# Hi/lo activation halves side by side in one 512-column product, low parts two ticks later, and w_up's row scale on VectorE

## Chip, cores and metric

The kernel runs on one core of a Trainium2 chip. The metric is the device time of one execution in microseconds; the median of three runs is given.

## The reference

One decoder block on 256 tokens of width 1024: a pooling mixer beside causal attention in 8 heads of 64, then cross attention with 4 heads of 256 on 256 memory tokens, then a feed-forward part of width 2816 with a causal convolution of three taps. All in float32.

```python
h = rms_norm(x, norm_mix_g); proj = h @ w_in                  # 1024 x 2048: pool part, q, k, v
x = x + concat([pool(u), attention(q, k, v)]) @ w_out
h = rms_norm(x, norm_xattn_g); m = rms_norm(mem, norm_mem_g)
q = rms_norm(h @ w_xq); k, v = split(m @ w_xkv); k = rms_norm(k)
x = x + softmax(q k^T / 16) v @ w_xo
h = rms_norm(x, norm_ffn_g)
up = conv3_causal(h @ w_up) + conv_b                          # 1024 x 5632
gate, val = split(up)
x = x + (silu(gate) * val) @ w_down                           # 2816 x 1024
```

## The kernel before, in words

Every large product keeps float32 accuracy with two-part operands: a value is a high part (rounded to the TensorE form fp32r) plus a low part (the rest), and a product is high x high + high x low + low x high. `split_h` (L186, ScalarE cast, L194) and `split_l` (L196, VectorE difference, L205) make both parts of a weight unit of 128x1024; `need(u)` (L207) calls them for units ahead of the one in use, by `look[0]` units. `LOOKS` sets that number for each stage, and `HOLD` sets it to 0 for the last tiles of a residual stage (3 tiles in the first, 1 in the second), so that the splits kept back come out in one go at the next stage's first `need`. Raw weights come by DMA in chunks of two units through three buffers.

There are two kinds of stages. In the first kind (`a_chunk`, L359: w_in and w_xkv) the activations are the stationary operand and 512 columns of weights stream. In the second kind, with transposed output (`b_tile`, L701: w_out, w_xq, w_xo, w_up, w_down), a 128x128 block of weights is stationary, the 256 tokens stream, and the output has its features on the partitions. There a block is three products of 256 columns by `three` (L263 to L267). One tile of 128 output features is 8 blocks (22 in w_down), accumulated in one PSUM bank or half of one. w_up runs 22 pairs of tiles (gate and value), 2 x 8 blocks each.

The order of all instructions is written out by hand. Work beside the products is in generators ("jobs"): `go` runs one to its first `yield`, `tick()` runs each living job one step further, and `wait(n)` is n yields. A tick comes after every second block inside a tile (not after its last) and one at the tile's end. Every engine executes its own instructions in the order in which they were issued; a position in that order is all that a `WAIT_...` number sets. `finish` ticks until certain jobs are done.

After each tile of w_out and w_xo, `resid_stage` (L712) adds the bank to the residual on VectorE (L719), makes the high part on ScalarE (L250) and the low part on VectorE (L256), both times the norm's gain, squares the residual on ScalarE (L725), and GpSimd adds the square to a running sum (L726). w_xq (L803) does the same without the residual; its squares come from the bank (L811). `x_job` (L745) is the cross attention of two heads, started some ticks after tiles 3 and 7 of w_xq; the value projection (L836) runs meanwhile. In w_up, `r2_job` (L861) forms the row scale 1/rms: a row sum on TensorE, `rsqrt` (L222, a seed on VectorE and 12 small GpSimd operations), a broadcast on TensorE, the copy `r2b` (L871), and then eight scaled activation tiles hs = resid x r2b on GpSimd (L881), split on ScalarE and VectorE. The first `SCALED` pairs of w_up work on the unscaled activations h2, and their result is multiplied by r2b on VectorE (L891); the rest work on hs. `up_job` (L885) is what follows each pair: ScalarE scales and shifts (L896, y), VectorE adds two taps for each half (L903), ScalarE's silu (L907), VectorE's product (L909), then the high part (L248) and the low part (L254) of act, which w_down reads. w_down's first tile waits for them one block after another.

## Time and profile before

| | us |
|---|---|
| median of three runs | 394.69 (394.58 to 394.85) |
| profiled execution | 395.07 |
| its span, first to last instruction | 393.3 |
| TensorE busy | 387.0 |
| VectorE busy | 283.1 |
| ScalarE busy | 231.5 |
| GpSimd busy | 90.0 |

The span is what the profile covers; the execution's time has some 1.8 us around it. A matmul's row in the profile overlaps the next one's, so a busy TensorE is read by the distance of the starts, not by the duration of one row. VectorE's and ScalarE's rows overlap their successors a little too.

### The profile page before, as it was taken

How to read it: one execution, taken by the hardware profiler on the slowest of the kernel's cores; microseconds unless marked ns; L12 is line 12 of the kernel's file. 1: busy time of each engine (PE TensorE's matmuls, PEld its weight loads, DVE VectorE, ACT ScalarE, POOL GpSimd, SP SyncE). 2: the span in 40 equal slices, each digit the busy share in tenths (PEclk: the TensorE clock that was granted, in tenths of full speed). 3: DMA queues.
4: the chain of work that ended last, by engine and by line, in shares of the span. 5: the costliest groups of instructions: out<-in, count | busy, mean ns of one | idle time of the engine just before them, and what ended most of it. 6: DMA issues, size and time to landing. Idle time of an engine off the chain costs nothing.

```text
span 393.3 us, 7301 instructions
## 1 busy us (share of the span) xinstructions
PE 387.0 (98%) x2898; PEld 367.2 (93%) x2898; DVE 283.1 (72%) x478; ACT 231.5 (59%) x421; POOL 90.0 (23%) x174
## 2 busy tenths in 40 slices
PE   8999999999999999999999999999999999999996
PEld 7878787889999998899999999999999999999996
DVE  4788989956876667857774999998877874543350
ACT  5775886957476556845555498765665576342300
POOL 0384883134441423001647300000000000000000
PEclk9999999999999999999999999999999999999999
DMA  8985372543336537242545226665465452455400
GB/s 273 422 342 207 119 304 72 166 190 108 109 107 222 208 107 262 76 198 107 202 143 197 105 108 227 243 249 177 176 213 180 161 197 108 135 227 176 173 21 19
DMA packets 12274, 69.22 MB, mean 176 GB/s; under 512 B 1360, under 2 KB 2768, under 8 KB 4688
## 3 DMA queue, kind: packets, MB, share of 16 engines
q1 hardware_dynamic: 11952, 68.24, 47.9%
q8 instruction: 22, 0.36, 0.4%
q10 hardware_dynamic: 288, 0.52, 0.4%
q14 instruction: 12, 0.10, 0.1%
HBM read 67.71 MB, written 1.05 MB: 175 GB/s over the span
## 4 chain that ended last, share of the span: by engine, by line
PE 80%; DVE 7%; DMA 5%; ACT 3%; POOL 2%; issue 2%; SPq 0%; DVEq 0%; POOLq 0%
PE bank L265 23%; PE bank L267 23%; PE bank L266 23%; DMA raw<-wpack 3%; PE bank L366 3%; PE bank L367 3%; PE bank L370 3%; DVE wl L205 2%; DMA sc<-xpack 1%; ACT wh L194 1%; DVE mg_l L256 1%; ACT sqx L300 0%; PE bank L677 0%; PE bank L795 0%; POOL rs3t L228 0%
## 5 line engine op out<-in xcount | busy, mean ns | idle before, releaser
L205 DVE TENSOR_TENSOR wl<-raw,wh 128x1024 fp32r<-128x1024 f32 (+1 forms) x126 | 150.3, 1209 | 5.4 <-ACT wh L194 5.3
L194 ACT CAST wh<-raw 128x1024 fp32r<-128x1024 f32 (+1 forms) x125 | 123.7, 1024 | 41.6 <-DMA raw<-wpack 41.0
L265 PE MATMUL bank<-hs_h,wh 128*128 128x256 f32 x288 | 81.5, 283 | 0.0
L266 PE MATMUL bank<-hs_l,wh 128*128 128x256 f32 x288 | 81.5, 283 | 0.0
L267 PE MATMUL bank<-hs_h,wl 128*128 128x256 f32 x288 | 81.5, 283 | 0.0
L265 PEld LDWEIGHTS bank<-hs_h,wh 128*128 128x128 f32 x288 | 55.3, 192 | 0.0
L266 PEld LDWEIGHTS bank<-hs_l,wh 128*128 128x128 f32 x288 | 55.3, 192 | 0.0
L267 PEld LDWEIGHTS bank<-hs_h,wl 128*128 128x128 f32 x288 | 55.3, 192 | 0.0
L265 PE MATMUL bank<-act_h,wh 128*128 128x256 f32 x176 | 49.8, 283 | 0.0
L266 PE MATMUL bank<-act_l,wh 128*128 128x256 f32 x176 | 49.8, 283 | 0.0
L267 PE MATMUL bank<-act_h,wl 128*128 128x256 f32 x176 | 49.8, 283 | 0.0
L903 DVE SCALAR_TENSOR_TENSOR y<-bank,sc,y 128x255 f32<-128x255 f32 (+1 forms) x72 | 29.8, 479 | 14.4 <-ACT y L896 14.4
L265 PE MATMUL bank<-h_h,wh 128*128 128x256 f32 x128 | 36.6, 286 | 0.0
L267 PE MATMUL bank<-h_h,wl 128*128 128x256 f32 x128 | 36.2, 283 | 0.0
L266 PE MATMUL bank<-h_l,wh 128*128 128x256 f32 x128 | 36.2, 283 | 0.0
L896 ACT ACTIVATE y<-bank,sc 128x256 f32<-128x256 f32 x36 | 18.3, 559 | 27.6 <-PE bank L267 27.6
L265 PEld LDWEIGHTS bank<-act_h,wh 128*128 128x128 f32 x176 | 33.8, 192 | 0.0
L266 PEld LDWEIGHTS bank<-act_l,wh 128*128 128x128 f32 x176 | 33.8, 192 | 0.0
L267 PEld LDWEIGHTS bank<-act_h,wl 128*128 128x128 f32 x176 | 33.8, 192 | 0.0
L946 DVE TENSOR_TENSOR o<-bank,sc 128x256 f32<-128x256 f32 x8 | 3.4, 425 | 35.2 <-PE bank L267 35.2
L366 PE MATMUL bank<-wh,mg_h 128*128 128x512 f32 x64 | 26.1, 408 | 0.0
L726 POOL TENSOR_TENSOR h_acc<-h_sq,h_acc 128x256 f32<-128x256 f32 x14 | 16.8, 1198 | 40.3 <-ACT h_sq L725 40.2
(244 smaller groups left out, 862.4 us busy)
## 6 DMA issues: line engine op xcount, KB each, us to landing
raw<-wpack SPq DMA_DIRECT2D x59, 1024.0 KB, 4.8
raw<-wpack SPq DMA_DIRECT2D x4, 512.0 KB, 7.7
mraw<-memT SPq DMA_DIRECT2D x4, 256.0 KB, 7.7
out<-o SPq DMA_DIRECT2D x8, 128.0 KB, 1.9
raw<-wpack ACTq DMA_DIRECT2D x2, 256.0 KB, 3.7
raw<-wpack SPq DMA_DIRECT2D x2, 256.0 KB, 4.7
sc<-xpack SPq DMA_DIRECT2D x1, 512.0 KB, 6.0
tab<-table SPq DMA_DIRECT2D x1, 480.0 KB, 9.7
```

The source lines that it names most:

```text
L194: copy(split[u][0][:, r], unit(u)[:, r])
L205: dve.tensor_tensor(l[:, r], unit(u)[:, r], h[:, r].bitcast(F32), op=ALU.subtract)
L256: dve.scalar_tensor_tensor(l, src, scale, h.bitcast(F32), op0=ALU.mult, op1=ALU.subtract)
L265: pe.matmul(o, stat[0], mov[0], start=start, stop=False)
L266: pe.matmul(o, stat[0], mov[1], start=False, stop=False)
L267: pe.matmul(o, stat[1], mov[0], start=False, stop=stop)
L366: pe.matmul(bk[tt], a[tt][0], wv[0], start=k == 0, stop=False)
L367: pe.matmul(bk[tt], a[tt][1], wv[0], start=False, stop=False)
L370: pe.matmul(bk[tt], a[tt][0], wv[1], start=False, stop=k == KT - 1)
L726: pool.tensor_tensor(acc, sq, acc, op=ALU.add)
L896: act.activation(y[:, g * S:(g + 1) * S], src[:, g * S:(g + 1) * S], AF.Identity, bias=col(sc, C_CB + f), scale=col(sc, C_CW + 2 * 2 * NFF ...
L903: dve.scalar_tensor_tensor(yy[:, j:], uu[:, :S - j], col(sc, C_CW + (2 - j) * 2 * NFF + f), yy[:, j:], op0=ALU.mult, op1=ALU.add)
```

## The change

- `pair` makes one tile that holds the high and the low part of a block side by side (256 + 256 columns), in place of two tiles. `tiles` returns the view of the high parts, that of the low parts, and one of both together.
- `both` takes the place of `three` in `b_tile`: one product of the weights' high part with the 512 columns [high | low], and one of the weights' low part with the 256 high columns, which adds into the first half of the bank. A tile now fills a whole bank, and its result is the sum of the bank's two halves.
- That sum is made when the bank is emptied: by two VectorE additions into the residual (`resid_stage`) and in the output; by a ScalarE copy of the second half to SBUF and a VectorE addition (w_xq, and each half in w_up). w_up takes two banks for a pair. What follows reads the sum from SBUF.
- In `resid_stage` and w_xq the low part comes out `WAIT_LOW` = 2 ticks after the rest of the tile's work.
- `rsqrt` in `r2_job` runs its three steps on VectorE, three operations each; `WAIT_R2` is shorter, and `SCALED` is 3 instead of 4. Every pair of w_up leaves its banks at once; the unscaled ones are multiplied by r2b in SBUF when r2b is there.
- `WAIT_R1` is 6 instead of 0.

The diff, without the places that only follow the new views:

```diff
--- before.py
+++ after.py
@@ -47,12 +47,13 @@
 WAIT_ATTN = [2, 6, 0]
 WAIT_POOL = [1, 6, 0, 7, 1, 5, 2, 6, 1]
 WAIT_KEY = [0, 4, 7, 2, 0, 13, 5]
-WAIT_R1 = [0]
+WAIT_R1 = [6]
 WAIT_X = [3, 0, 0, 0, 10, 0, 6, 13, 8]
 WAIT_VALUE = [32]
-WAIT_R2 = [6, 11, 2, 2, 0]
+WAIT_R2 = [6, 6, 1, 1, 0]
+WAIT_LOW = [2]
 WAIT_UP = [6, 2, 5, 7, 9, 8]
-SCALED = 4
+SCALED = 3
 WARM = 10
 
 
@@ -100,9 +101,8 @@
         return temps.tile([P, S], F32, name=name, tag="t1", bufs=8)
 
     def pair(name, cols=KT * S):
-        h = pairs.tile([P, cols], F32R, name=name + "_h", tag="ph", bufs=4)
-        l = pairs.tile([P, cols], F32R, name=name + "_l", tag="pl", bufs=4)
-        return h, l
+
+        return pairs.tile([P, 2 * cols], F32R, name=name, tag="pair", bufs=4)
 
     def sm(name, n, dtype=F32):
         return small.tile([P, n], dtype, name=name)
@@ -219,12 +219,17 @@
 
     cnt = [0]
 
-    def rsqrt(x, n):
+    def rsqrt(x, n, quick=False):
 
         cnt[0] += 1
         y, t = sm(f"rs{cnt[0]}y", n), sm(f"rs{cnt[0]}t", n)
         dve.tensor_scalar(y.bitcast(I32), x.bitcast(I32), -0.5, float(0x5F3759DF), op0=ALU.mult, op1=ALU.add)
         for _ in range(3):
+            if quick:
+                dve.tensor_tensor(t, y, y, op=ALU.mult)
+                dve.scalar_tensor_tensor(t, t, -0.5, x, op0=ALU.mult, op1=ALU.mult)
+                dve.scalar_tensor_tensor(y, t, 1.5, y, op0=ALU.add, op1=ALU.mult)
+                continue
             pool.tensor_tensor(t, y, y, op=ALU.mult)
             pool.tensor_tensor(t, t, x, op=ALU.mult)
             pool.tensor_scalar(t, t, -0.5, 1.5, op0=ALU.mult, op1=ALU.add)
@@ -266,11 +271,25 @@
         pe.matmul(o, stat[0], mov[1], start=False, stop=False)
         pe.matmul(o, stat[1], mov[0], start=False, stop=stop)
 
+    def both(b, stat, mov, start, stop):
+
+        n = mov.shape[1] // 2
+        if start:
+            pe.matmul(b, stat[0], mov, start=True, stop=False)
+            pe.matmul(b[:, 0:n], stat[1], mov[:, 0:n], start=False, stop=False)
+        else:
+            pe.matmul(b[:, 0:n], stat[1], mov[:, 0:n], start=False, stop=False)
+            pe.matmul(b, stat[0], mov, start=False, stop=stop)
+
     def col(t, c):
         return t[:, c:c + 1]
 
-    def tiles(p, k=KT):
-        return [t.rearrange("p (k s) -> p k s", k=k) for t in p]
+    def tiles(t, *dims):
+
+        names = " ".join("abc"[:len(dims) - 1])
+        sizes = dict(zip("abc", dims[:-1]))
+        v = t.rearrange(f"p ({names} z s) -> p z {names} s", z=2, **sizes)
+        return v[:, 0], v[:, 1], t.rearrange(f"p ({names} w) -> p {names} w", **sizes)
 
     rows = {}
 
...
@@ -704,26 +723,34 @@
             i = f * blocks + k
             w = need(u0 + i // 8)
             wv = [t[:, (i % 8) * P:(i % 8 + 1) * P] for t in w]
-            three(b, wv, mov(k), k == 0, k == blocks - 1)
+            both(b, wv, mov(k), k == 0, k == blocks - 1)
             halves[0] += 1
             if halves[0] % 2 == 0 and k < blocks - 1:
                 tick()
 
     def resid_stage(u0, actv, gain, name, phase, held):
-        hv = tiles(pair(name))
+        hv = tiles(pair(name), KT, S)
         acc = t1(name + "_acc")
-        for f in range(KT):
-            b = bank()[:, 0:S]
-            look[0] = HOLD[2] if f >= KT - HOLD[held] else LOOKS[phase]
-            b_tile(u0, f, KT, b, lambda k: [t[:, k] for t in actv])
-            dve.tensor_tensor(resid[:, f], b, resid[:, f], op=ALU.add)
-            evac_split(hv[0][:, f], hv[1][:, f], resid[:, f], col(sc, gain + f))
+
+        def empty(f, b):
+            for z in range(2):
+                dve.tensor_tensor(resid[:, f], b[:, z * S:(z + 1) * S], resid[:, f], op=ALU.add)
+            g = col(sc, gain + f)
+            part_h(hv[0][:, f], resid[:, f], g)
             if f == 0:
                 act.activation(acc, resid[:, f], AF.Square)
             else:
                 sq = t1(f"{name}_sq{f}")
                 act.activation(sq, resid[:, f], AF.Square)
                 pool.tensor_tensor(acc, sq, acc, op=ALU.add)
+            yield from wait(WAIT_LOW[0])
+            part_l(hv[1][:, f], resid[:, f], hv[0][:, f], g)
+
+        for f in range(KT):
+            b = bank()
+            look[0] = HOLD[2] if f >= KT - HOLD[held] else LOOKS[phase]
+            b_tile(u0, f, KT, b, lambda k: actv[2][:, k])
+            go(empty(f, b))
             tick()
         look[0] = LOOKS[phase + 1]
         return hv, acc
...
@@ -799,20 +826,28 @@
             part_l(ptv[1][:, h], bb, ptv[0][:, h])
         yield from wait(WAIT_X[7])
 
-    jobs_x = []
-    for f in range(KT):
-        b = bank()[:, 0:S]
-        b_tile(34, f, KT, b, lambda k: [t[:, k] for t in h1])
-        if f == 0:
-            job_r1.append(go(r1_job()))
-        part_h(xqv[0][:, f], b, col(ggx, f % 2))
-        part_l(xqv[1][:, f], b, xqv[0][:, f], col(ggx, f % 2))
+    def xq_empty(f, b):
+        q = t1(f"xq{f}")
+        act.copy(q, b[:, S:])
+        dve.tensor_tensor(q, b[:, 0:S], q, op=ALU.add)
+        g = col(ggx, f % 2)
+        part_h(xqv[0][:, f], q, g)
         sq = t1(f"xsq{f}")
-        act.activation(sq, b, AF.Square)
+        act.activation(sq, q, AF.Square)
         if f % 2 == 0:
             sqp[f // 2] = sq
         else:
             pool.tensor_tensor(sqp[f // 2], sq, sqp[f // 2], op=ALU.add)
+        yield from wait(WAIT_LOW[0])
+        part_l(xqv[1][:, f], q, xqv[0][:, f], g)
+
+    jobs_x = []
+    for f in range(KT):
+        b = bank()
+        b_tile(34, f, KT, b, lambda k: h1[2][:, k])
+        if f == 0:
+            job_r1.append(go(r1_job()))
+        go(xq_empty(f, b))
         tick()
         if f % 4 == 3:
             def x_start(hp):
...
@@ -862,7 +897,7 @@
 
         yield from wait(WAIT_R2[0])
         v2 = yield from row_mean(acc2, "2")
-        r2 = rsqrt(v2, TT)
+        r2 = rsqrt(v2, TT, True)
         yield from wait(WAIT_R2[1])
         b = bank()
         for tt in range(TT):
@@ -882,14 +917,17 @@
                 prev = t
             yield from wait(WAIT_R2[4])
 
-    def up_job(i, b, scaled):
-        src = b
+    def up_job(i, bs, scaled):
+        src = t2(f"up{i}")
+        for g in range(2):
+            half = src[:, g * S:(g + 1) * S]
+            act.copy(half, bs[g][:, S:])
+            dve.tensor_tensor(half, bs[g][:, 0:S], half, op=ALU.add)
         if not scaled:
             while not r2_ready:
                 yield
-            src = t2(f"up{i}")
-            dve.tensor_tensor(src.rearrange("p (g s) -> p g s", g=2), b.rearrange("p (g s) -> p g s", g=2),
-                              r2b[:, None, :].to_broadcast([P, 2, S]), op=ALU.mult)
+            src2 = src.rearrange("p (g s) -> p g s", g=2)
+            dve.tensor_tensor(src2, src2, r2b[:, None, :].to_broadcast([P, 2, S]), op=ALU.mult)
         y = t2(f"y{i}")
         for g in range(2):
             f = i + g * NFF
...
@@ -917,33 +955,34 @@
     jobs_up = []
     look[0] = LOOKS[10]
     for i in range(NFF):
-        b = bank()
+        bs = [bank(), bank()]
         if i == 0:
-            hs2 = tiles(pair("hs2"))
+            hs2 = tiles(pair("hs2"), KT, S)
             job_r2.append(go(r2_job()))
         scaled = i >= SCALED
         hv = hs2 if scaled else h2
         if i == SCALED:
             finish(job_r2[0])
         for g in range(2):
-            b_tile(58, 2 * i + g, KT, b[:, g * S:(g + 1) * S], lambda k: [t[:, k] for t in hv])
+            b_tile(58, 2 * i + g, KT, bs[g], lambda k: hv[2][:, k])
             if g == 0:
                 tick()
         if i % 8 == 0:
-            acts.append(tiles(pair(f"act{i // 8}")))
-        jobs_up.append(go(up_job(i, b, scaled)))
+            acts.append(tiles(pair(f"act{i // 8}"), KT, S))
+        jobs_up.append(go(up_job(i, bs, scaled)))
         tick()
 
     def act_tile(k):
         finish(jobs_up[k])
-        return [t[:, k % 8] for t in acts[k // 8]]
+        return acts[k // 8][2][:, k % 8]
 
     look[0] = LOOKS[11]
     for f in range(KT):
-        b = bank()[:, 0:S]
+        b = bank()
         b_tile(102, f, NFF, b, act_tile)
         o = t2(f"o{f}")[:, 0:S]
-        dve.tensor_tensor(o, b, resid[:, f], op=ALU.add)
+        for z, add in enumerate((resid[:, f], o)):
+            dve.tensor_tensor(o, b[:, z * S:(z + 1) * S], add, op=ALU.add)
         nc.sync.dma_start(out[:, f], o)
 
 
```

## Rows read from the trace of the kernel before

**Rows 1.** The page: busy time of TensorE, and the granted TensorE clock in 40 slices of the span.
```profile
PE 387.0 (98%) x2898; PEld 367.2 (93%) x2898; DVE 283.1 (72%) x478; ACT 231.5 (59%) x421; POOL 90.0 (23%) x174
...
PEclk9999999999999999999999999999999999999999
```

**Rows 2.** Waits of TensorE for other engines, longest first: who for whom, us in total, times, longest.
```profile
PE bank L332 <- DVE idle L329: 1.1, 1, 1.1
```

**Rows 3.** Products of w_up on the scaled activations and of w_down, one row for one of the three products of each block: count, duration of one in ns (min/median/max), first and last start in us.
```profile
L266 PE MATMUL bank<-hs_l,wh x288: 283/283/283, 222.7 to 326.1; 128*128 128x256 f32 x144
...
L265 PE MATMUL bank<-act_h,wh x176: 283/283/283, 326.3 to 389.3; 128*128 128x256 f32 x176
```

**Rows 4.** Timeline of TensorE in the value projection, products of 512 columns: start us, us, engine, line, operation.
```profile
159.44 0.39 PE L366 MATMUL bank<-wh,mg_h 128*128 128x512 f32 x1
...
160.35 0.62 PE L370 MATMUL bank<-wl,mg_h 128*128 128x512 f32 x2
160.80 0.39 PE L366 MATMUL bank<-wh,mg_h 128*128 128x512 f32 x1
```

**Rows 5.** Groups of instructions by form: one of the three products of the blocks on h (w_xq and the first four pairs of w_up), cat (w_out) and ox (w_xo); count | busy us, mean ns.
```profile
L265 PE MATMUL bank<-h_h,wh 128*128 128x256 f32 x128 | 36.6, 286 | 0.0
...
L265 PE MATMUL bank<-cat_h,wh 128*128 128x256 f32 x64 | 18.4, 288 | 0.4 <-DVE cat_l L256 0.4
...
L265 PE MATMUL bank<-ox_h,wh 128*128 128x256 f32 x64 | 18.1, 283 | 0.0
```

**Rows 6.** Timeline of VectorE in the steady part of w_up, one pair of tiles (in brackets: idle time before, and what ended it).
```profile
269.95 1.65 DVE L903 SCALAR_TENSOR_TENSOR y<-bank,sc,y 128x255 f32<-128x255 f32 x4 [1.17 <-ACT y L896]
271.52 1.22 DVE L205 TENSOR_TENSOR wl<-raw,wh 128x1024 fp32r<-128x1024 f32 x1
272.65 0.42 DVE L909 TENSOR_TENSOR sg<-sg,y 128x256 f32<-128x256 f32 x1
272.99 0.42 DVE L254 TENSOR_TENSOR act_l<-sg,act_h 128x256 fp32r<-128x256 f32 x1
273.32 1.22 DVE L205 TENSOR_TENSOR wl<-raw,wh 128x1024 fp32r<-128x1024 f32 x1
275.71 1.65 DVE L903 SCALAR_TENSOR_TENSOR y<-bank,sc,y 128x255 f32<-128x255 f32 x4 [1.17 <-ACT y L896]
```

**Rows 7.** The same operation in two pairs earlier in w_up, where VectorE has no idle time.
```profile
250.22 1.66 DVE L903 SCALAR_TENSOR_TENSOR y<-bank,sc,y 128x255 f32<-128x255 f32 x4
...
254.72 1.66 DVE L903 SCALAR_TENSOR_TENSOR y<-bank,sc,y 128x255 f32<-128x255 f32 x4
```

**Rows 8.** Timeline of VectorE: four operations in a row with one operand in PSUM; then, by form, the residual addition, and a ScalarE copy of 128x256 from PSUM.
```profile
91.00 1.41 DVE L254 TENSOR_TENSOR cat_l<-bank,cat_h 128x256 fp32r<-128x256 f32 x4
...
L719 DVE TENSOR_TENSOR sc<-bank,sc 128x256 f32<-128x256 f32 x16 | 6.7, 420 | 3.3 <-PE bank L267 3.2
...
L558 ACT COPY pt<-bank 128x256 f32<-128x256 f32 x4 | 1.5, 387 | 0.0
```

**Rows 9.** Timelines at the start of w_up: VectorE, then ScalarE, then GpSimd.
```profile
198.90 0.42 DVE L719 TENSOR_TENSOR sc<-bank,sc 128x256 f32<-128x256 f32 x1 [1.39 <-PE bank L267]
...
204.45 0.17 DVE L226 TENSOR_SCALAR rs9y<-v 128x2 int32<-128x2 int32 x1
...
212.02 0.42 DVE L871 COPY r2b<-bank 128x256 f32<-128x256 f32 x1 [2.76 <-PE bank L869]
...
216.67 4.88 DVE L256 SCALAR_TENSOR_TENSOR hs_l<-hs,sc,hs_h 128x256 fp32r<-128x256 f32 x8 [1.63 <-ACT hs_h L250]
...
199.36 0.51 ACT L250 ACTIVATE h_h<-sc 128x256 fp32r<-128x256 f32 x1 [2.06 <-DVE sc L719]
199.78 0.40 ACT L725 ACTIVATE h_sq<-sc 128x256 f32<-128x256 f32 x1
200.09 3.88 ACT L194 CAST wh<-raw 128x1024 fp32r<-128x1024 f32 x4
...
210.50 0.20 POOL L231 TENSOR_TENSOR rs9y<-rs9t,rs9y 128x2 f32<-128x2 f32 x1
212.53 7.16 POOL L881 TENSOR_TENSOR hs<-sc,r2b 128x256 f32<-128x256 f32 x8 [1.83 <-DVE r2b L871]
```

**Rows 10.** Timelines at the start of w_xq: VectorE behind the last tile of w_out, and the transposes on TensorE.
```profile
114.98 0.42 DVE L719 TENSOR_TENSOR sc<-bank,sc 128x256 f32<-128x256 f32 x1 [0.38 <-PE bank L267]
...
116.39 0.68 DVE L254 TENSOR_TENSOR kx_l<-bank,kx_h 128x512 fp32r<-128x512 f32 x1
116.99 2.38 DVE L205 TENSOR_TENSOR wl<-raw,wh 128x1024 fp32r<-128x1024 f32 x2
...
116.94 0.60 PE L677 MATMUL bank<-tab,kn 128*128 128x128 f32 x4
```

**Rows 11.** Timelines behind w_xq: the last xq_h on ScalarE, the last xq_l on VectorE, and the first product of the second head pair on TensorE.
```profile
145.00 0.48 ACT L250 ACTIVATE xq_h<-bank,ggx 128x256 fp32r<-128x256 f32 x1
...
145.88 0.48 DVE L256 SCALAR_TENSOR_TENSOR xq_l<-bank,ggx,xq_h 128x256 fp32r<-128x256 f32 x1
...
148.29 0.36 PE L265 MATMUL bank<-kx_h,xq_h 128*128 128x256 f32 x1
```

**Rows 12.** The last act_l (first and last start in us), and the output's addition by form.
```profile
L254 DVE TENSOR_TENSOR act_l<-sg,act_h x22: 418/421/433, 242.1 to 330.8; 128x256 fp32r<-128x256 f32 x22
...
L946 DVE TENSOR_TENSOR o<-bank,sc 128x256 f32<-128x256 f32 x8 | 3.4, 425 | 35.2 <-PE bank L267 35.2
```

More of the change, by code (lines that the diff above doesn't have):

```diff
@@ L447, in qk_job @@
         yield from wait(WAIT_QK[5])
-    qk = pairs.tile([P, KT * S], F32, name="qkT", tag="ph", bufs=4)
+    qk = pairs.tile([P, KT * S], F32, name="qkT", tag="pair", bufs=4)
     j_of = {"q": 0, "k": 1}
@@ L592, in block_kernel @@
     a_chunk(12, xgv, bu)
-    cat = tiles(pair("cat"))
+    cat = tiles(pair("cat"), KT, S)
     def pool_job():
@@ L689, in block_kernel @@
     finish(job_k)
-    kxv = tiles(pair("kx"))
+    kxv = tiles(pair("kx"), KT, S)
     job_key0 = go(key_job(0, bk0))
@@ L788, in x_job @@
         if not ptv:
-            ptv.extend(t.rearrange("p (h m q) -> p h m q", h=XH, m=TT) for t in pair("xpt"))
+            ptv.extend(tiles(pair("xpt"), XH, TT, S))
         for j, h in enumerate(hs):
@@ L836, in block_kernel @@
     a_chunk(42, mgv, bv0)
-    vxv = [t.rearrange("p (m d) -> p m d", m=TT) for t in pair("vx")]
+    vxv = tiles(pair("vx"), TT, XH * XD)
     go(value_job(0, bv0))
@@ L840, in block_kernel @@
     a_chunk(46, mgv, bv1)
-    oxv = tiles(pair("ox"))
+    oxv = tiles(pair("ox"), KT, S)
     finish(*jobs_x)
```

20 lines of the change are left out of this document (10 added, 10 removed).

## The prediction

> **What bounds the kernel now.** I read the page's busy rows first, then what TensorE waits for, then the stretches of the timeline in which a stage begins. TensorE is busy for 98% of the span at the full granted clock, 1.0 in every slice [rows 1], and its longest wait for another engine is 1.1 us [rows 2]. In the last two stages the products follow one another without a hole: the 288 blocks of w_up on the scaled activations start between 222.7 and 326.1 us, the 176 of w_down between 326.3 and 389.3 us [rows 3]. So a microsecond taken from TensorE counts in full, as long as VectorE and ScalarE deliver in time. That is the second thing to read: VectorE has the least room in w_up.
>
> **TensorE.** A block (one 128x128 weight tile on 256 tokens) is three products of 256 columns. 287 intervals in 103.4 us make 0.360 us for a block, 0.120 for a product [rows 3]. Six products of 512 columns take 160.80 - 159.44 = 1.36 us, 0.227 each [rows 4]. Twice as many columns cost 0.107 more, so 0.0134 us of each product does not depend on its columns. The new block is one of 512 and one of 256: 0.227 + 0.120 = 0.347 us, 0.0134 less. No row shows the two in turn; the bounds are nothing saved (0.360) and the 0.0134, and I take the latter, since both forms show the same remainder. Blocks: 352 in w_up, 176 in w_down, 64 each in w_out, w_xq and w_xo [rows 3, 5], together 720. 720 x 0.0134 = 9.7 us off the path.
>
> The Trainium skill speaks against this term: "TensorE: Matmul & The Clock Gate", section Back-to-back issue gap, gives a warm gap of N/2.4 + 2.5 ns, so dropping one product would save 2.5 ns, 1.8 us in all. The rows say otherwise: 120 ns where that rule has 109. I go by the rows.
>
> **What the second half costs VectorE in w_up.** In the steady part one pair of tiles takes 5.76 us on TensorE, and VectorE stands idle for 1.17 us of it, waiting for ScalarE's y [rows 6]. When VectorE was behind, the same work went through in 254.72 - 250.22 = 4.50 us [rows 7]. New are two additions of 128x256 for each pair. Four such operations with a PSUM operand took 1.41 us, that is (1.41 - 0.42)/3 = 0.33 each in a row [rows 8]; alone they last 0.42 [rows 8]. So VectorE needs 4.50 + 0.67 = 5.17 us (5.34 at the upper end) for a pair that TensorE now does in 16 x 0.347 = 5.55. It fits, with 0.2 to 0.4 us to spare in place of 1.2. ScalarE gets two copies a pair, 0.39 us each [rows 8]; at 59% of the span [rows 1] it has the room.
>
> **Delayed low parts: three new holes.** A low part now goes out two ticks after its tile. The first tick is the one at the tile's end, the second comes after the second block of the next tile, behind the weight splits that this tile's first block orders. Inside a stage that is harmless, the next stage being far off. For the last tile (f = 7) it is not: the next stage needs that low part in its eighth block, and the block now needs it in its 512-column product.
> - Into w_up. TensorE starts about 198.7 us; VectorE's addition of f = 7 comes at 198.90 [rows 9]. New chain, from TensorE's start: two additions 0.2 to 1.0; h_h 1.1 to 1.6 (0.51); the square, whose successor starts 0.31 after it, to 1.9; the cast of weight unit 62 to 2.9 (3.88 us for four, 0.95 in a row [rows 9]); the differences of units 61 and 62, the second after that cast, to 4.1 (1.13 in a row [rows 6]); the low part to 4.55. Needed: 7 x 0.347 + 0.12 = 2.55. TensorE stands for 2.0 us (1.0 to 2.7).
> - Into w_xq. The same chain, with kx_l and two differences behind the addition [rows 10]: ready at 4.6. Four transposes (about 0.5 us) stand before the eighth block [rows 10], so it is needed at 3.0: 1.6 us (0.6 to 2.5).
> - Behind w_xq. Here f = 7 is evacuated late, because ScalarE first does the four exponentials of the first head pair: xq_h started at 145.00 [rows 11]. Now a copy and an addition come before it (about 1.5 us with the additions' place in VectorE's queue and 0.3 for the low part of f = 6), and three weight differences before the low part, the last of which waits for the second cast: copy at 145.3, h 146.65, square to 147.45, two casts to 149.35, difference to 150.55, low part ready at 151.1. The products of the second head pair begin at 148.29 [rows 11] and the twelfth needs it, at 149.6: 1.6 us (0 to 2.5).
> No DMA instruction is moved; the loads stand at the same splits.
>
> **Row scale, SCALED = 3.** rsqrt drops 12 GpSimd operations, which end at 210.7, 6 us after VectorE's seed [rows 9], and puts 9 small ones on VectorE, 0.17 to 0.2 each [rows 9]: 1.8 us. GpSimd's eight products follow r2b; they began at 212.53 and took 7.2 us [rows 9]. With TensorE's hole above, r2b comes about 12 us after the stage's start (13.3 before), and the last hs_l at 20 to 20.5. The scaled blocks now begin after 48 blocks instead of 64: 48 x 0.347 + 2.0 + 0.9 (row sum and broadcast on TensorE, my estimate from rows 10) = 19.6, the eighth at 22: no wait. But VectorE stands in its queue at hs_l behind GpSimd for about 7 us, with the additions of pair 1, the row scale of pairs 0 and 1, and the weight differences queued behind it. I follow that queue from 20.5: a row scale 0.6, about 1.5 for ScalarE's y and copies, two additions 0.7, a row scale 0.6, the difference of unit 66 1.1, the taps of pairs 0 and 1 3.1 (0.39 each [rows 6]), the difference of unit 67 1.1: ready at 29.2. It is needed in block 72, at 72 x 0.347 + 2.9 + 0.2 = 28.1. GpSimd may be quicker while VectorE stands, so I take 0.7 us for this hole (0 to 2). From there VectorE gains 0.38 us a pair on a backlog of about 7 us, so it catches up only near the end. The last act_l started at 330.8, and its block at 326.3 + 21 x 0.36 = 333.9 [rows 3, 12]. Now VectorE has, behind the last hs_l, 40 differences at 1.13, 88 taps at 0.39, 42 additions and 44 products and low parts at 0.33 and three row scales at 0.6, together 110 us [rows 6, 8]; with 1.5 of waits it ends at 132. The block comes at 373 x 0.347 + 2.9 + 0.7 = 133: about 1 us is left. I book 0.3 us (0 to 3).
>
> **Tail.** The output takes two additions in place of one of 0.42 us [rows 12], the second dependent on the first: 0.4 us.
>
> **Sum.** -9.7 + 2.0 + 1.6 + 1.6 + 0.7 + 0.3 + 0.4 = -3.1 us on the profiled span of 393.3, so 390.2. The profiled execution took 395.07 with 1.8 us around the span; the median of the runs is 394.69. Taking 3.0 us from that gives 391.7.
>
> **The rivals.**
> - VectorE becomes the bound in w_up, and the change loses. Place: the chain copy, addition, y, tap operation now crosses between ScalarE and VectorE three times for a pair, and in the steady rows VectorE already stands for 1.17 us at this place [rows 6]. For it: 5.17 against 5.55 leaves little. Against it: one weight difference now stands between the additions and the taps, and it covers y. If VectorE still stands 0.35 us a pair from pair 3 on, that is 19 x 0.35 = 6.7, less the 1 us of margin: 5.6 us more, 397.3 us. It makes the kernel slower than before once it stands longer than (1.0 + 3.0)/19 = 0.21 us a pair.
> - The holes at the stages' starts are not there, because the low parts arrive earlier than my chain has them. Then 9.7 - 0.4 - 0.5 is left: 385.9 us. Against it: that order is fixed in each engine's queue, and each link has a row.
> - The two products in turn save nothing that a row of one form shows. The extreme is the saving of 1.8 us from the skill's rule: -1.8 + 6.6 = +4.8, 399.5 us. For it: no row mixes the forms. Against it: rows 3 and 4 give the same 0.0134 us for both.
> - TensorE's clock falls in the new holes. The rows have no hole over 1.1 us behind which to look [rows 2]; a clock of 1.2 GHz for the 4 us that follow costs 2 us each time. It is in the upper end of the range.
>
> **Chances.** Forecast 0.60, with a range of its own of 389.3 to 394.3; VectorE bound 0.18; no holes 0.14; no saving for each product 0.05; clock 0.03. A run of this kernel can tell about 0.2%, 0.8 us, from no change. Faster: 0.50 of the forecast, 0.14, and 0.01 = 0.65. Same: 0.06 + 0.04 + 0.02 = 0.12. Slower: 0.23. The range of 387.0 to 396.2 leaves out most of the case without holes and the worse half of the VectorE case.
>
> **What would show it.** Right: products starting 0.227 and 0.120 us apart in w_down, whose 176 blocks then take 61.0 us; waits of TensorE for the low parts of h1, xq and h2, each once, 1.5 to 2 us; VectorE without a pause from about 20 us after the start of w_up until near its end, and then a small one. Wrong: a block that still takes 0.36 us; TensorE waiting for weight differences again and again in w_up, or for act_l at the first tile of w_down; no waits at the stages' starts.

## The result, and the profile after

| | before | after |
|---|---|---|
| median of the runs beside each other | 394.77 us (4 runs) | 397.83 us (4 runs, 396.8 to 398.35) |
| ratio, 95% interval | | 1.0069 [1.005, 1.0088] |
| profiled execution, its span | 395.07, 393.3 | 397.58, 395.8 |

The change makes the kernel 0.7% slower; I had forecast 0.8% faster. The profiled execution lost 2.5 us where the sum said 3.1 gained.

The page of the changed kernel, the lines that answer to [rows 1], with VectorE's busy share in 40 slices:

```profile
PE 383.2 (97%) x2178; PEld 328.8 (83%) x2178; DVE 312.3 (79%) x562; ACT 247.7 (63%) x473; POOL 79.8 (20%) x162
...
DVE  4788989957985858677976989999999999564461
...
PEclk9999999999998999999999999999999999999999
```

720 products fewer, and VectorE has 29 us more to do, in an unbroken stretch of nines from about 237 us to the end of w_up. The slice of the clock that is no longer a 9 is the thirteenth, at about 120 us.

TensorE's waits, longest first, answer to [rows 2]:

```profile
PE bank L282 <- DVE h L261: 4.2, 2, 2.4
PE bank L272 <- DVE xq L261: 1.5, 1, 1.5
```

The three holes stand at the starts of w_xq and w_up and of the second head pair, each for a low part; none is for act. Nor does this view list a wait for a weight difference in w_up, but the starts show two short ones, in the tiles of units 68 and 69 (the eleventh and twelfth of w_up). These took 3.14 and 3.05 us where others of their speed take 2.78 and 2.82: 0.6 us late in sum. The first two products of the eleventh tile, 0.47 us apart in place of 0.23, and VectorE's difference, which ends at 234.45, just ahead of the second:

```profile
234.03 0.40 PE L278 MATMUL bank<-hs,wh 128*128 128x512 f32 x1
234.50 0.38 PE L279 MATMUL bank<-hs,wl 128*128 128x256 f32 x1
233.23 1.22 DVE L205 TENSOR_TENSOR wl<-raw,wh 128x1024 fp32r<-128x1024 f32 x1
```

"Late tiles" below are read in this way, by the length of a tile against others of its speed. On the timeline of TensorE, the product after the first hole and the blocks that follow it:

```profile
117.43 0.28 PE L281 MATMUL bank<-h,wl 128*128 128x256 f32 x1
120.09 0.50 PE L282 MATMUL bank<-h,wh 128*128 128x512 f32 x1 [2.38 <-DVE h L261]
...
121.87 0.63 PE L282 MATMUL bank<-h,wh 128*128 128x512 f32 x1
...
122.51 0.63 PE L282 MATMUL bank<-h,wh 128*128 128x512 f32 x1
...
124.20 0.40 PE L282 MATMUL bank<-h,wh 128*128 128x512 f32 x1
...
124.55 0.40 PE L282 MATMUL bank<-h,wh 128*128 128x512 f32 x1
```

Behind the hole the blocks stand 0.64 us apart, and 0.35 only from 124.2 on. The windows of the same stretch show why (window; its length and the busy time of PE, PEld, DVE, ACT, POOL; granted clock, DMA share, GB/s):

```profile
117.00:120.00 3.00, 0.70 (x6) 0.39 (x3) 2.91 (x4) 1.85 (x3) 0.96 (x1) 1.00 0.46 131
120.00:121.00 1.00, 0.91 (x3) 0.78 (x4) 0.03 (x1) 0.32 (x1) 0.00 (x0) 0.74 1.02 434
121.00:122.00 1.00, 1.00 (x6) 0.90 (x5) 0.92 (x2) 0.51 (x3) 0.00 (x0) 0.50 0.53 221
...
123.00:124.00 1.00, 1.00 (x5) 0.90 (x4) 0.03 (x1) 0.30 (x1) 0.00 (x0) 0.56 0.48 66
124.00:125.00 1.00, 1.00 (x6) 0.82 (x6) 0.00 (x0) 0.00 (x0) 0.00 (x0) 1.00 0.61 213
```

TensorE stood for 2.38 us, and its granted clock then was 0.50, that is 1.2 GHz, for some 3.4 us (120.5 to 123.9); half of that, 1.7 us, is lost besides the hole.

The block itself, in w_down, answers to [rows 3]: TensorE's timeline in the first tile, then in a later one.

```profile
331.22 0.39 PE L282 MATMUL bank<-act,wh 128*128 128x512 f32 x1
...
332.95 0.40 PE L282 MATMUL bank<-act,wh 128*128 128x512 f32 x1
...
361.11 0.40 PE L282 MATMUL bank<-act,wh 128*128 128x512 f32 x1
...
362.17 0.40 PE L282 MATMUL bank<-act,wh 128*128 128x512 f32 x1
```

Five blocks in 1.73 us are 0.346 each; three in 1.06 are 0.353. Where nothing comes between, every tile of the stages with transposed output runs at one of these two speeds from its second block to its last: w_down's first tile at 0.347 and the other seven at 0.353. In w_xo and in the steady part of w_up the two take turns tile by tile, and a pair of tiles takes 5.593 us from start to start, 0.3496 a block. (The 304 blocks of w_up on hs took 106.87 us, 0.3515 each, but this average holds the two late tiles.) The 176 blocks of w_down took 61.77 us to the start of the last product, 0.3523 each.

VectorE in the steady part of w_up answers to [rows 6]; its timeline, one pair of tiles:

```profile
289.25 0.41 DVE L259 TENSOR_TENSOR act<-sg,act 128x256 fp32r<-128x256 f32 x1
289.58 0.74 DVE L925 TENSOR_TENSOR up<-bank,up 128x256 f32<-128x256 f32 x2
290.25 1.21 DVE L205 TENSOR_TENSOR wl<-raw,wh 128x1024 fp32r<-128x1024 f32 x1
291.38 1.66 DVE L941 SCALAR_TENSOR_TENSOR y<-up,sc,y 128x255 f32<-128x255 f32 x4
292.96 1.21 DVE L205 TENSOR_TENSOR wl<-raw,wh 128x1024 fp32r<-128x1024 f32 x1
294.10 0.41 DVE L947 TENSOR_TENSOR sg<-sg,y 128x256 f32<-128x256 f32 x1
294.43 0.41 DVE L259 TENSOR_TENSOR act<-sg,act 128x256 fp32r<-128x256 f32 x1
```

A pair takes it 5.18 us without a pause, and TensorE 5.59.

Where the time went, by stages (us from a stage's first product to the next one's, last column to the start of the kernel's last product; E5 and E9 are experiments below):

| | up to w_out | w_out | w_xq | value | av | w_xo | w_up | w_down | w_out to the end |
|---|---|---|---|---|---|---|---|---|---|
| before | 90.36 | 24.42 | 27.68 | 27.45 | 5.75 | 23.04 | 127.60 | 63.24 | 299.18 |
| after | 90.74 | 23.81 | 31.20 | 29.20 | 5.76 | 22.37 | 126.63 | 61.77 | 300.74 |
| E5 | 92.03 | 23.82 | 27.58 | 27.42 | 5.75 | 22.37 | 125.84 | 61.90 | 294.68 |
| E9 | 89.88 | 23.73 | 27.65 | 27.46 | 5.75 | 22.31 | 125.49 | 61.08 | 293.47 |

The first part, which the change hardly touches, differs by a microsecond or two between executions, so experiments are compared below by the last column as well as by their medians. After the change w_xq (+3.5) and the value stage (+1.75) lost more than all others gained.

### The profile page after: what moved, and what is told of

The parts are those of the page before. It is cut to its first block, busy times and chain, and to the rows that moved or that the text cites. A ratio compares the mean times of both kernels' runs of the same rounds, so it can differ in the third digit from the quotient of the medians.

```text
span 395.8 us, 5983 instructions
## 1 busy us (share of the span) xinstructions
PE 383.2 (97%) x2178; PEld 328.8 (83%) x2178; DVE 312.3 (79%) x562; ACT 247.7 (63%) x473; POOL 79.8 (20%) x162
## 4 chain that ended last, share of the span: by engine, by line
PE 62%; DVE 18%; ACT 7%; POOL 5%; issue 4%; DMA 3%; SPq 0%; DVEq 0%; ACTq 0%; POOLq 0%
PE bank L282 30%; PE bank L281 15%; DVE wl L205 5%; PE bank L278 3%; PE bank L385 2%; DMA raw<-wpack 2%; PE bank L386 2%; PE bank L389 2%; ACT wh L194 2%; PE bank L279 2%; DVE hs L261 1%; DMA sc<-xpack 1%; DVE sc L737 1%; DVE h L261 1%; PE bank L272 1%
## 5 line engine op out<-in xcount | busy, mean ns | idle before, releaser
L282 PE MATMUL bank<-hs,wh 128*128 128x512 f32 x266 | 94.8, 396 | 0.0
L281 PE MATMUL bank<-hs,wl 128*128 128x256 f32 x266 | 74.2, 279 | 0.0
L282 PE MATMUL bank<-act,wh 128*128 128x512 f32 x168 | 59.6, 398 | 0.0
L282 PEld LDWEIGHTS bank<-hs,wh 128*128 128x128 f32 x266 | 49.9, 188 | 10.3
L281 PEld LDWEIGHTS bank<-hs,wl 128*128 128x128 f32 x266 | 50.1, 189 | 1.6
L281 PE MATMUL bank<-act,wl 128*128 128x256 f32 x168 | 47.1, 281 | 0.0
L282 PE MATMUL bank<-h,wh 128*128 128x512 f32 x98 | 36.5, 407 | 4.2 <-DVE h L261 4.2
L934 ACT ACTIVATE y<-up,sc 128x256 f32<-128x256 f32 x44 | 24.1, 595 | 26.3 <-DVE up L925 19.6
L941 DVE SCALAR_TENSOR_TENSOR y<-up,sc,y 128x255 f32<-128x255 f32 (+1 forms) x88 | 36.5, 473 | 0.3 <-ACT y L934 0.3
L985 DVE TENSOR_TENSOR o<-bank,sc 128x256 f32<-128x256 f32 x8 | 3.4, 425 | 29.4 <-PE bank L282 29.4
L385 PE MATMUL bank<-wh,mg 128*128 128x512 f32 x64 | 26.1, 408 | 0.0
L385 PE MATMUL bank<-wh,xg 128*128 128x512 f32 x64 | 25.6, 399 | 0.3 <-ACT xg L255 0.2
L386 PE MATMUL bank<-wh,mg 128*128 128x512 f32 x64 | 25.1, 392 | 0.0
L386 PE MATMUL bank<-wh,xg 128*128 128x512 f32 x64 | 25.0, 391 | 0.0
L255 ACT ACTIVATE h<-sc 128x256 fp32r<-128x256 f32 x16 | 8.2, 511 | 20.5 <-DVE sc L737 20.5
```

The source lines that it names most:

```text
L255: act.activation(h, src, AF.Copy, scale=scale)
L281: pe.matmul(b[:, 0:n], stat[1], mov[:, 0:n], start=False, stop=False)
L282: pe.matmul(b, stat[0], mov, start=False, stop=stop)
L385: pe.matmul(bk[tt], a[tt][0], wv[0], start=k == 0, stop=False)
L386: pe.matmul(bk[tt], a[tt][1], wv[0], start=False, stop=False)
L934: act.activation(y[:, g * S:(g + 1) * S], src[:, g * S:(g + 1) * S], AF.Identity, bias=col(sc, C_CB + f), scale=col(sc, C_CW + 2 * 2 * NFF ...
```

## The experiments

My theory after the result: the three holes of the delayed low parts, and TensorE's clock behind them, eat a saving that is itself smaller than forecast. The rivals: VectorE, now without a pause, is what costs; the wide product saves next to nothing; the quick row scale loses.

**E1, low parts after one tick.**

```diff
-WAIT_LOW = [2]
+WAIT_LOW = [1]
```

> The changed kernel with WAIT_LOW = 1: each low part goes out at the tick at its tile's end, ahead of the weight splits of the next tile; all else is unchanged. Theory (three holes of TensorE at the stages' starts and a slower clock behind the longest of them cost 7.5 us): TensorE no longer waits for the low parts of h1, xq and h2 (2.4 + 1.5 + 1.8 us in the changed kernel), the granted clock stays at 1.0 (1.8 us), time about 390.5 us. Rival (VectorE, without a pause from 240 to 336 us in the changed kernel, is the bound in w_up, and the holes only gave it time): what the holes give back is lost again in w_up, in waits for weight differences or for act, time 395 us or more.

393.4 us, ratio to before 0.9963 [0.9951, 0.9975]; w_out to the end 296.87. The holes are gone, but for 0.6 us at w_xq's start, and the kernel is faster than before, though less than expected. TensorE's waits:

```profile
PE bank L279 <- DVE wl L205: 1.6, 3, 0.9
```

In place of the holes it waits for weight differences: VectorE's additions of f = 7 now come 2.2 us after w_xq's start (115.94, with the start at 113.75), where the changed kernel has them at 0.2 (114.75 and 114.55), and the differences behind them come late. In w_up, too, tiles come late here by 2.0 us in sum (units 66, 68 and 69; the longest wait is the 0.9 for unit 68), against 0.6 in the changed kernel, where TensorE starts later by its hole of 1.8 us into w_up.

**E2, always the 512-column product first.** Both branches of `both` become one; no two products of a size meet at a border of tiles any more.

```diff
-        if start:
-            pe.matmul(b, stat[0], mov, start=True, stop=False)
...
+        pe.matmul(b, stat[0], mov, start=start, stop=False)
+        pe.matmul(b[:, 0:n], stat[1], mov[:, 0:n], start=False, stop=stop)
```

> The changed kernel with one order in every block: the 512-column product first, then the 256-column one, so that two products of one kind never meet at a tile's border. In the changed kernel the blocks of a tile follow each other either at 0.3467 or at 0.3533 us, the same throughout a tile, and in the 8-block stages by turns. Theory (the two speeds come from how the sequence begins in a tile, at the border where equal kinds meet): all tiles at 0.3467, some 3 us less, about 394.5 us. Rival (the two speeds have another cause, such as the bank or the address): both speeds stay, time as the changed kernel, about 397.8 us.

397.56 us (395.87 to 401.02), w_out to the end 302.98. The rival came out, in the time and in that both speeds stay; but they no longer go by tiles. The blocks of w_up run at 0.347 from the row scale's broadcast (215 us) to two late weight differences at 235 and 238 us, over seven tiles and their borders, and at 0.353 from 240 us to the end of w_down; in w_xq four tiles run at 0.347. Two starts in w_up, sixteen blocks apart:

```profile
219.26 0.40 PE L277 MATMUL bank<-h,wh 128*128 128x512 f32 x1
224.80 0.40 PE L277 MATMUL bank<-hs,wh 128*128 128x512 f32 x1
```

So neither speed needs a border of two equal products. Without such borders the stream keeps a speed from tile to tile, and changes it only behind a hole, a wait or other products; that over thirty tiles in a row keep one speed speaks against the bank as its cause. The fall of the clock came in another place, behind the 2.03 us hole into w_up, and not behind the 2.9 us one into w_xq.

**E3, three products again.** The 512-column product is made as two of 256 (but in a tile's first block); banks, additions and delays stay.

```diff
-            pe.matmul(b, stat[0], mov, start=False, stop=stop)
+            pe.matmul(b[:, 0:n], stat[0], mov[:, 0:n], start=False, stop=False)
+            pe.matmul(b[:, n:], stat[0], mov[:, n:], start=False, stop=stop)
```

> The changed kernel with the 512-column product split again into two of 256 columns, in all blocks but the first of each tile; banks, additions and delays stay. Theory (the wide product is worth about 0.0085 us a block, as the changed kernel's blocks take 0.3515 on average and 0.360 before): 7 of 8 blocks at 0.360, some 5.5 us more, 403 us, holes a little shorter. Rival (the wide product brings nothing): 397.8 us.

401.28 us (1.0166 [1.0152, 1.018]), w_out to the end 304.65, without a fall of the clock. So the wide product alone is worth 3.9 us in the changed kernel as profiled, some 5.5 if its fall of the clock is left out, though the changed kernel's holes are longer by 0.5 us and two of its tiles come late. The rival that mixed products save nothing is out.

**E4, the old row scale** (GpSimd's rsqrt, four unscaled pairs).

```diff
-WAIT_R2 = [6, 6, 1, 1, 0]
+WAIT_R2 = [6, 11, 2, 2, 0]
-SCALED = 3
+SCALED = 4
-        r2 = rsqrt(v2, TT, True)
+        r2 = rsqrt(v2, TT)
```

> The changed kernel with the row scale of before: rsqrt's steps on GpSimd, the old WAIT_R2 numbers, SCALED = 4. Theory (the row scale's place costs nothing, since TensorE has no wait there): within 0.6 us of the changed kernel, 397.8 us. Rival (VectorE standing behind GpSimd's products earlier, or the earlier scaled pairs, cost time): 396.5 us or less. If the quick row scale is what keeps VectorE in time: more than 399 us, with waits of TensorE in the first pairs of w_up.

399.86 us (1.0119 [1.0095, 1.0143]), w_out to the end 302.14: the quick row scale helps, by 2.0 us between the two ratios, and w_up took 2.3 us more without it (128.93). The last of the three expectations came out, with the waits in the sixth and seventh pair. TensorE's waits and the product behind the first hole, with the windows there:

```profile
PE bank L282 <- DVE h L261: 4.8, 2, 2.9
PE bank L279 <- DVE wl L205: 2.0, 3, 1.2
```

```profile
120.14 0.51 PE L282 MATMUL bank<-h,wh 128*128 128x512 f32 x1 [2.93 <-DVE h L261]
```

```profile
118.00:120.00 2.00, 0.00 (x0) 0.00 (x0) 2.00 (x3) 0.90 (x2) 0.00 (x1) 1.00 0.67 193
120.00:122.00 2.00, 1.86 (x10) 1.64 (x11) 0.94 (x3) 0.77 (x2) 0.00 (x0) 1.00 0.79 332
```

With the later scale TensorE waits 2.0 us for weight differences, 32 to 42 us after w_up's start. And a longer hole than the changed kernel's has a clock of 1.00 behind it: w_xq took 30.21 - 2.93 = 27.28 us without its hole, the changed kernel's 31.20 - 2.38 = 28.82. The difference, 1.54, prices the fall a second time.

**E5, one tick for the last tile alone.** The delay inside a stage stays, f = 7 gets one tick (in `resid_stage` and in `xq_empty`).

```diff
-            yield from wait(WAIT_LOW[0])
+            yield from wait(1 if f == KT - 1 else 2)
```

> The changed kernel, with the low part delayed two ticks inside a stage as before, and by one tick only for the last tile (f = 7) of w_out, w_xq and w_xo. If the low part of f = 7 alone makes the holes at the stages' starts, and the delay inside a stage is what keeps VectorE from being late, it takes the holes of 2.4, 1.5 and 1.85 us away without the 1.2 us of lateness that one tick everywhere brought: TensorE then waits at most about 0.6 us at each start, and the time is 391 to 392.5 us, below the 393.4 of one tick everywhere. Rival: the weight differences that now stand behind the low part are late by as much as it is early; then it is like one tick everywhere, 393 to 394 us, with waits for wl of 1.5 us in sum.

391.56 us, ratio to before 0.9914 [0.9887, 0.9941]; w_out to the end 294.68, 6.1 less than the changed kernel's. The longest of TensorE's waits that are left:

```profile
PE bank L279 <- DVE wl L205: 1.2, 2, 1.0
PE bank L351 <- DVE idle L348: 1.1, 1, 1.1
```

Three of the 24 delayed low parts, moved by one tick, turn a loss of 3 us into a gain of 3. The changed kernel's three holes (5.7 us) and its fall of the clock (1.6), less 1.3 for w_up's late tiles (1.9 us here, 0.6 there), make 6.0 of the 6.1.

**E6, the two products in turns.** h, l, then l, h, then h, l: equal sizes meet at each border of blocks.

```diff
-        if start:
+        flip[0] = 0 if start else 1 - flip[0]
+        if flip[0] == 0:
```

> The changed kernel, with the two products of a block in turns: h then l, l then h, h then l, so that at every border of two blocks products of the same kind meet (512, 256, 256, 512, 512, 256 ...) in place of 512, 256, 512, 256. If the slower of the two block times (0.3533 us; the other is 0.3467) comes of a strict alternation of the two sizes, every tile runs at 0.3467, w_down takes 61.0 in place of 61.8 us and w_up 1.4 us less: 395.5 us, with the holes as they are. If the slower time belongs to the sizes themselves or to the address of the bank or of the activations, half the tiles stay at 0.353 and the time at 397.8. A third way out, each change of size costing something: there are half as many, so blocks of 0.340 and 393 us.

399.91 us, but not for the blocks; TensorE's timeline in w_down:

```profile
360.09 0.39 PE L281 MATMUL bank<-act,wh 128*128 128x512 f32 x1
360.32 0.28 PE L282 MATMUL bank<-act,wl 128*128 128x256 f32 x1
360.43 0.28 PE L284 MATMUL bank<-act,wl 128*128 128x256 f32 x1
360.55 0.40 PE L285 MATMUL bank<-act,wh 128*128 128x512 f32 x1
...
362.18 0.40 PE L281 MATMUL bank<-act,wh 128*128 128x512 f32 x1
```

Six blocks in 2.09 us are 0.348, in every tile, and w_down took 61.07 us, as the first theory said. The time went to the holes: 3.0 us into w_xq (it was 2.4 and 2.9 in the changed kernel and E4, which are the same up to there), and in the profiled execution the clock fell to 0.50 behind this hole and again behind that into w_up; the runs show mean clocks of 0.983 to 0.991.

**E7, two more VectorE operations a pair in w_up.**

```diff
+            dve.tensor_tensor(half, half, half, op=ALU.max)
```

> The changed kernel, with one further VectorE operation of 128x256 behind each of the two additions of a pair in w_up (the maximum of the sum with itself, which changes nothing), two a pair, 0.33 us each in a row. VectorE needed 5.17 us a pair by my sum where TensorE takes 5.62 (16 x 0.3515). If that sum is right, 5.84 is more than 5.62, VectorE becomes the bound in w_up, and TensorE waits for wl or act there: some 18 pairs x 0.22 + the margin of about 1.5 us used up, 400 to 402 us. Rival: VectorE has more room than the sum says (its pauses were only backlog worked off), and the time stays within 0.6 us of 397.8.

417.27 us, 19.4 more than the changed kernel, far above what I expected. VectorE's timeline, one pair of tiles, and TensorE's waits:

```profile
281.69 0.42 DVE L259 TENSOR_TENSOR act<-sg,act 128x256 fp32r<-128x256 f32 x1
282.02 0.42 DVE L925 TENSOR_TENSOR up<-bank,up 128x256 f32<-128x256 f32 x1
282.48 0.43 DVE L926 TENSOR_TENSOR up<-up 128x256 f32<-128x256 f32 x1
282.82 0.42 DVE L925 TENSOR_TENSOR up<-bank,up 128x256 f32<-128x256 f32 x1
...
287.80 0.42 DVE L259 TENSOR_TENSOR act<-sg,act 128x256 fp32r<-128x256 f32 x1
```

```profile
PE bank L282 <- DVE act L259: 6.2, 2, 3.6
PE bank L279 <- DVE wl L205: 5.2, 15, 1.8
```

A pair takes VectorE 6.11 us in place of 5.18, 0.465 for each added operation and not the 0.33 of [rows 8]: the maximum reads the addition ahead of it and starts 0.46 us behind it, the next addition 0.34 behind the maximum. Over 22 pairs that is 20.5 us. The last low part of act starts 153.4 us after w_up's start (354.4), in the changed kernel 132.4 (335.5): 21.0 later; w_up and w_down together became 21.1 longer, a fall of the clock behind the last waits included. So VectorE's work in w_up is a path of its own beside TensorE's, with the 1.2 us to spare that the changed kernel has before act's last block in w_down's first tile, and what goes beyond them comes out at the end in full. My expectation counted only the excess of a steady pair over TensorE's; but VectorE works off a backlog from the first pair to the last.

Up to w_up this kernel is the changed one, and its hole into w_xq is as long (2.38 us), but no fall of the clock follows: w_xq took 29.63 us, 1.57 less. It did fall behind the 1.8 us hole into w_up.

**E8, the delay alone.** The kernel before, with three products, and the low parts of h1, xq and h2 after two ticks.

```diff
-            evac_split(hv[0][:, f], hv[1][:, f], resid[:, f], col(sc, gain + f))
+            part_h(hv[0][:, f], resid[:, f], g)
...
+            yield from wait(2)
+            part_l(hv[1][:, f], resid[:, f], hv[0][:, f], g)
```

> The kernel before (three products of 256 columns in each block), with nothing of the change but the two ticks of delay for the low parts of h1, xq and h2. If the delay alone makes the holes, TensorE waits for h, xq and h at the three starts, by 1 to 2 us each: less than in the changed kernel by the second addition and the copy, and because a 256-column low product needs the low part one product later: 3 to 4.5 us in sum, 398 to 399.5 us with none or one fall of the TensorE clock behind a hole. Rival: the holes come of the additions and copies ahead of the low part; then it stays within 1 us of 394.8.

399.82 us (1.0133 [1.0091, 1.0175]). TensorE's first wait:

```profile
PE bank L266 <- DVE h_l L256: 3.2, 2, 1.8
```

The delay costs the old kernel 3.7 us in the profiled execution (302.86 against 299.18) and 5.0 by the medians, at clocks of 0.991 to 0.998 in the runs. The hole behind w_xq isn't there (27.44 for the value stage): the last low part of xq is done 7.0 us after the stage's start, in time. In the changed kernel, with a copy and an addition ahead of it, that is 8.8 us.

**E9, E5 and E6 together.**

> The two edits that helped put together: the low part of a stage's last tile after one tick, and the two products of a block in turns (512, 256, 256, 512), which made every block 0.348 us. From 391.6 us with the first alone: the 192 blocks of w_out, w_xq and w_xo gain 0.6 us, w_down 0.8, w_up's 352 blocks 1.2 if VectorE keeps up: 389.0 to 390 us, with no hole over 1 us at the starts of w_xq and w_up. Rival: in w_up VectorE (5.18 us a pair against 16 x 0.348 = 5.57, with its backlog) is the bound as soon as TensorE is quicker; then w_up's share comes back as waits for wl or for act at the first tile of w_down, and the time is 390.5 us or more.

389.67 us (389.46 to 390.05), ratio to before 0.9862 [0.9839, 0.9884]: the fastest version, 1.4% under the kernel before. TensorE's first wait:

```profile
PE bank L282 <- DVE wl L205: 1.5, 3, 1.0
```

w_down gained 0.82 on E5. w_up gained 0.35. The 1.2 expected there came of the average of 0.3515; a steady pair went from 5.593 to 5.573 us, which is 0.44 in 22 pairs, and the late tiles cost 2.0 us in place of 1.9. So the VectorE rival took back less than 0.1.

**E10, the third tap left out** (on E5; the output lacks that tap): `for j in (1,)` in place of `(1, 2)`.

> The kernel with one tick for the last tile's low part (391.6 us), with the third tap of the convolution left out: 44 of 88 VectorE operations of 0.39 us in w_up, two a pair. So the output lacks that tap. If the 1.2 us that TensorE still waits for wl at the start of w_up are VectorE's backlog, they go (by half at least, since the taps of the first pairs lie ahead of the weight difference that is waited for): 390.3 to 391.0 us. Rival: the difference is late for another reason (its cast on ScalarE, its DMA); then the time stays at 391.6.

389.56 us; w_out to the end 293.55, 1.13 less than E5 (of the 3.1 between the two profiled executions the rest lies before w_out). The waits for wl fell from 1.2 to 0.8; 0.27 of either is in w_xq, and w_up's late tiles cost 0.8 us in place of 1.9. So more than half of what E5 still loses in w_up is VectorE's backlog.

**E11, the holes filled with idle products.** On the changed kernel; 9 and 7 of the start-up's products ahead of the eighth block.

```diff
+            if k == KT - 1 and (u0, f) in FILL:
+                spare = bank()
+                for _ in range(FILL[u0, f]):
+                    pe.matmul(spare[:, 0:P], idle, idle, start=True, stop=True)
```

> The changed kernel, with products of the idle tile on TensorE (their result is not used) put into its two holes: nine ahead of the eighth block of the first tile of w_xq and seven ahead of that of w_up, 0.214 us each by the profile's first rows, so 1.9 and 1.5 us, less than the holes. The holes stay as long; only their idle time is filled. If the fall of TensorE's clock to 1.2 GHz comes of the idle time, no slice of the profile falls under 0.95, w_xq takes 29.4 in place of 31.2 us, and the median of the runs goes from 397.8 to 396 to 396.8. Rival: the fall has nothing to do with the idle time; then clock and median stay at 0.990 to 0.996 and 397.8.

396.81 us (1.0051 [1.003, 1.0073]); the interval overlaps the changed kernel's. What can be read are the twelve runs: six at mean clocks of 0.997 to 1.0 took 395.8 to 396.3 us, four at 0.994 to 0.996 took 397.3 to 397.5, two at 0.990 and 0.993 took 399.3 and 399.8. None of the changed kernel's four runs had a clock over 0.996. Falls may have become rarer, and one costs about 1.3 us; that idle time alone makes them isn't shown, since 0.9 us of the first hole and the 1.5 us hole behind w_xq stayed. The w_xq stage took 30.24 us and not the 29.4 expected: the hole there, its filled part included, was some 2.9 us in this execution.

**E12, three products in w_up alone** (on E5, without copies and additions there).

> The kernel with one tick for the last tile's low part (391.6 us), with three products of 256 columns again in w_up alone, and without the copies and additions there; w_out, w_xq, w_xo and w_down keep the 512-column product. By the block times 352 x 0.0085 = 3.0 us are lost; if the 1.2 us of waits for wl come of VectorE's two additions a pair, they go, and what is left is 1.8: 393.4 us. Rival: what VectorE and ScalarE pay in w_up takes the whole gain there; then the time is 391.6 or less.

392.77 us (0.9942 [0.9925, 0.9959]), w_out to the end 296.38, 1.7 more than E5. A steady pair takes 5.760 us here, so by E5's 5.593 the wide product saves 3.7 us in w_up's 22 pairs, not the 3.0 of the average, and 1.7 of it arrive. E5's late tiles (1.9 us) are gone; the waits for wl are 0.3, all in w_xq. So the copies and additions cost some 1.9 us in w_up, not the whole gain.

## Why the prediction was wrong

The sum against the profiled execution (us):

| term | forecast | measured |
|---|---|---|
| 720 blocks | -9.7 | -7.0 |
| hole into w_xq | 1.6 | 2.4 |
| hole behind w_xq | 1.6 | 1.5 |
| hole into w_up | 2.0 | 1.8 |
| fall of TensorE's clock | 0 (a rival, 0.03) | 1.6 |
| VectorE late with unit 67 | 0.7 | 0.6 (units 68, 69) |
| act at w_down's first tile | 0.3 | 0 |
| tail | 0.4 | 0.6 |
| the rest, 0.4 of it before w_out | | 1.0 |
| sum | -3.1 | 2.5 |

**The step that failed most is the first: the saving of a block was mis-sized, 0.0097 us measured on average in place of 0.0134.** It was 0.0104 in the stages of eight blocks (0.360 less 0.3496) and 0.0077 in w_down (0.360 less 0.3523): 7.0 us in place of 9.7. The 0.0085 that the expectations of E3 and E12 go by holds the late tiles besides. I had bounds of nothing and 0.0134 and took the upper end, because 256-column and 512-column products by themselves show the same remainder. They do; but in turn they show it only in the fast tiles, 0.347 us a block. In the slow ones, 0.353, half of the saving is gone, and E6 gets nearly all of it back by the order of the two products alone. The Trainium skill's rule on this ("TensorE: Matmul & The Clock Gate", Back-to-back issue gap) would make a block (512 + 256)/2.4 + 5 = 325 ns, an estimate; neither speed agrees with it. What makes one tile fast and the next slow stays open. E2 shows that neither speed needs a border of equal products, and the tiles of w_down that run slow at its end, where VectorE is nearly idle, speak against its load.

**The second is the clock, which I left out of the sum.** Three holes of 1.6 to 2.0 us were in my own forecast, each longer than any in the trace of before, and I gave the fall behind them 0.03. It lasted 3.4 us, not the 4 of my rival, and cost 1.5 to 1.7 us in the profiled execution. It doesn't follow each hole: 2.38 us with a fall and 2.38 without (E7), 2.93 us without one (E4), 2.9 without and 2.03 with (E2). In the profiled executions of the changed kernel, E2 to E4 and E6 to E8 it followed 5 of these 20 holes. The Trainium skill (the same page, What's actually happening) has a monitor that lowers the clock after little activity and that runs free of the program; the falls that come and go between executions agree with that. A chance well above 0.03 for each hole would have been the honest reading of "no row to look at"; one in four, as in these executions, would have put 1.2 us in the sum.

**The holes: right in mechanism.** E8 shows that the delay makes those into w_xq and w_up, and E5 that the last tile's low part is all of it. The third goes with the delay too (E5), but the delay alone doesn't make it (E8); that the copy and the addition do the rest is what my chain says, and no run takes them alone. `WAIT_R1` = 6, which the forecast left out, was not tested either. The one into w_xq was 0.8 too small. VectorE's timeline there:

```profile
114.75 0.89 DVE L737 TENSOR_TENSOR sc<-bank,sc 128x256 f32<-128x256 f32 x2
115.55 0.68 DVE L259 TENSOR_TENSOR kx<-bank,kx 128x512 fp32r<-128x512 f32 x1
116.15 2.89 DVE L205 TENSOR_TENSOR wl<-raw,wh 128x1024 fp32r<-128x1024 f32 x2
118.96 0.68 DVE L259 TENSOR_TENSOR kx<-bank,kx 128x512 fp32r<-128x512 f32 x1
119.56 0.47 DVE L261 SCALAR_TENSOR_TENSOR h<-sc,h 128x256 fp32r<-128x256 f32 x1
```

My chain had one kx and two differences ahead of the low part; a second kx (0.6) stands there as well, which I had not followed, and the differences ended 0.3 later. The low part is done 5.5 us after TensorE's start (114.55), not 4.6.

**VectorE in w_up: right, to a hundredth.** 5.17 us a pair forecast, 5.18 measured; no pause in the steady pairs; the last low part of act was done at 335.9, 1.2 us before the product that reads it, where I had 1 us. The rival with VectorE as the bound did not come about in the changed kernel; that its 397.3 us lies near the measured 397.83 is chance. But E7 shows how near it was: some 1.2 us in the whole of w_up. In the faster versions VectorE's late differences cost 1.9 to 2.0 us there (E5, E9).

**Row scale and tail.** The scaled blocks began 19.8 us after the stage's start (forecast 19.6). The wait of 0.7 us behind it came one unit later than I had it, as 0.6 us at units 68 and 69, and is larger once the hole before it is gone (2.0 in E1, 1.9 in E5). I gave the quick scale no gain of its own; E4 makes it some 2 us.

Had the terms been right, the sum would have shown the change as a loss, and the way out: 7.0 us saved, 7.3 us of holes and clock paid for a delay that the last tile of each stage doesn't need, and 1.2 for late differences and the tail.

## What to carry to other kernels

A delay that is free inside a stage is paid in full at the stage's last tile; give that tile its own number, as E5 does, before judging the change as a whole. When a price is known only for two forms of an instruction apart, don't take the upper bound for the two in turn, and try the order in which they alternate. Compare the length of a tile with that of its like: short waits show there that a list of waits leaves out, and an average over a stage hides them. When a forecast contains holes longer than any in the trace, it contains a possible fall of TensorE's clock for each of them.

## What the runs showed of the hardware

- Two block speeds for the same instructions, 0.347 and 0.353 us, constant inside a tile, and 0.348 everywhere when the 512- and 256-column products are ordered so that equal sizes meet at each border of blocks (E6). In strict alternation a speed lasted over seven tiles, until the stream was interrupted (E2). The cause is open.
- Behind holes of 1.8 to 3.0 us TensorE's granted clock fell to 0.50 for some 3.4 us in some executions, and stayed at 1.00 behind equal or longer holes in others (2.38 us with and without, the changed kernel and E7).
- A VectorE operation of 128x256 starts 0.46 us behind the one whose result it reads, against 0.33 to 0.34 for independent ones (E7).
